# Hybrid decoder block on one core: gate and up as one level of Strassen's product, down as a stage of its own, full-height indexer matmuls

## The chip, the core and the metric

The kernel runs on one NeuronCore of one Trainium2 chip. A core has a matmul engine (TensorE, "PE" in the profile, with its weight loads listed as "PEld"), three elementwise engines (VectorE "DVE", ScalarE "ACT", GpSimd "POOL") and DMA queues, of which SyncE's ("SP") carries nearly all the transfers here. Every engine executes its own list of instructions in order; engines wait for each other through semaphores. The metric is the device time of one execution in microseconds (us). Lower is better.

## What is computed

The reference is one decoder block on 1024 tokens of width 1024, all in float32. What matters here is its last sub-layer and one piece of its first:

```
def _swiglu(h, w_gate_up, w_down):                 # D_FF = 2816
    g, u = jnp.split(h @ w_gate_up, 2, axis=-1)
    return (jax.nn.silu(g) * u) @ w_down
...
x = x + _rmsnorm(_swiglu(_rmsnorm(x, norm_ffn_pre), w_gate_up, w_down), norm_ffn_post)
...
dots = einsum('bthd,bsd->bths', q_idx, k_idx)      # indexer: 4 heads of 64 channels
score = einsum('bths,bth->bts', relu(dots), w_idx) # then top 256 keys per query
```

Ahead of the feed-forward layer stand the mixer sub-layer (one wide projection, causal pooling, the indexer with its top-256 selection, sparse attention, gating) and a cross-attention over 256 memory tokens.

## The kernel before

**Three matmuls for one product.** Every float32 operand is split into a high part of the reduced type `fp32r` and the rest, `lo = x - hi`. `split` (line 369) does it with one ACT copy and one DVE subtraction; `mm3` (line 425) then multiplies hi·hi, hi·lo and lo·hi, three matmuls of the fast type, into one PSUM bank. `wcols` and `wsplit` (lines 408 to 423) load and split a 128-column stripe of weights. So each product of a 128x128 weight block and 512 tokens is three 128x512 matmuls.

**The order is planned, not written.** `Recorder` (lines 54 to 329) collects every instruction with what it reads and writes, gives each a cost (`_cost`, line 185), and plays a list schedule: whichever engine is free takes the earliest recorded instruction that is ready by the model's clock and has room for its tiles. The result is one fixed order for each engine. Costs only decide this order. Big SBUF tiles (4 KB in each partition) come from one pool of `NSLOT` = 39 slots (tag "b", line 352); an instruction that opens such a tile may be taken at most `AHEAD` = 700 (or `SHORT` = 200) instructions ahead of the oldest one not yet planned. Four buffers of tag "ld" hold loads; PSUM is four single banks and two pairs of banks.

**The indexer** (lines 542 to 595). `kih` holds the high part of the keys in rows 0 to 63 and a copy in rows 64 to 127; `qi[h]` holds a head's high part in one half of the rows and its low part in the other; the copies between halves are DMAs issued from POOL (lines 552, 553, 564). `do_scores` then does one matmul over all 128 rows, which gives hi·hi + lo·hi, and one over 64 rows (`qi[h][pr]`, `kil[pr]`, line 587), which adds hi·lo, for each segment of keys. ACT applies the relu and DVE the weighted sum. The top-256 search that follows runs on DVE in the background of later projections.

**The end of the memory sub-layer.** `mem_out(b)` (line 1004) makes the 24 matmuls of token block b (tile `z`); `close` (line 930) is the chain that follows: ACT sums squares (`j_pb`), POOL makes the factor, DVE applies it (`zb`), POOL adds the residual (`zb` again), ACT sums squares (`j_nb`), POOL makes the factor, DVE applies it (`xn_nb`), and `norm_T` (line 444) makes eight PE transposes (`pt_nb`) whose result is split into `h3T`, the FFN's input: hidden channels by tokens, in two halves of 512 tokens (`HalfT`, line 455). Half 0 needs blocks 0 to 3 only.

**The feed-forward layer** (lines 1042 to 1105). For each stripe f of the 22 stripes of 128 hidden columns: gate (`o_g`), two token halves of 8 chunks by three matmuls, silu on ACT, the same for up (`o_up`), the product on DVE, a split into `aT`. After two stripes (four for the last piece) the `dn` matmuls multiply them with the rows of `w_down` and DVE adds the result to eight accumulators `acc`. The last piece also normalises, adds the residual and stores.

Of the kernel before, what the change touches and what calls it, by code (L numbers as in the profile page):

```python
# [10 lines left out]
F32 = mybir.dt.float32  # L11
F32R = mybir.dt.float32r
# [5 lines left out]
P = 128  # L18
# [35 lines left out]
class Recorder:  # L54
# [286 lines left out]
def hybrid_block_kernel(ctx: ExitStack, tc: tile.TileContext, x, mem, norm_mix_pre, norm_mix_post,  # L341
# [24 lines left out]
    def f32(t):  # L366
        return t.bitcast(F32)
# [76 lines left out]
    def norm_T(src, g, dst, name, eng=None):  # L444
        r = rstd_of(src, name)
        xn = slot([P, D], F32, f"xn_{name}")
        apply_norm(xn, src, r, g, eng)
        for q in range(2):
            pt = bank([P, 4, P], f"pt_{name}{q}")
            for c in range(4):  # L450
                nc.tensor.transpose(pt[:, c], xn[:, (4 * q + c) * P:(4 * q + c + 1) * P], ident)
            for (hi, lo, a, b) in dst(q):
                split(hi, lo, pt[:, a:b])

    class HalfT:
# [21 lines left out]
        def tok(self, b, c):  # L477
            h, t = divmod(b, 4)
            s = slice(t * P, (t + 1) * P)
            return self.hi[h][c // 2][:, c % 2, s], self.lo[h][c // 2][:, c % 2, s]  # L480

    class QuartT:
        def __init__(self, name):
            self.hi = [[None] * 2 for _ in range(4)]
# [59 lines left out]
    kih, kil = slot([P, S], F32R, "kih"), slot([P, S], F32R, "kil")  # L544
    qi = [slot([P, S], F32R, f"qi{m}") for m in range(IDXH)]
    for h in range(2):
        o = gemm_half(*wki[0], hT, h, "ki", (0, 512) if h else (0, 256, 512))
        s = slice(h * 512, (h + 1) * 512)
        nc.scalar.activation(kih[:64, s], o[:64], AF.Copy)
        nc.vector.tensor_tensor(kil[:64, s], o[:64], f32(kih[:64, s]), op=OP.subtract)  # L550
# [24 lines left out]
    def do_scores(i):  # L575
        n = (i + 1) * P
        off, segs = qk_cols(n)
        sc = slot([P, S], F32, f"score{i}")
        score[i] = sc
        qs = slice(i * P, (i + 1) * P)  # L580
        for h in range(IDXH):
            pr = slice((h % 2) * 64, (h % 2) * 64 + 64)
# [12 lines left out]
        nc.gpsimd.affine_select(sc[:, i * P:n], sc[:, i * P:n], pattern=[[-1, P]], compare_op=OP.is_ge,  # L595
                                fill=LOW, base=0, channel_multiplier=1)
# [331 lines left out]
                mm3(o[:, n], ah, al, w[c][0][:, ns], w[c][1][:, ns], c == 0, c == nk - 1)  # L928

    def close(o, res, dram, b, gpost, gpre, dst, name):  # L930
        of = o.rearrange("p n f -> p (n f)")
# [25 lines left out]
    h3T = HalfT("h3")  # L957
    oT = {}

    def mem_soft(u):  # L960
# [78 lines left out]
    pend()  # L1039


    g6 = gain(norm_ffn_post, "g6")
    acc = [None] * NB
    NF = DFF // P
    pieces = [range(f, f + 2) for f in range(0, NF - 4, 2)] + [range(NF - 4, NF)]
    for fs in pieces:
        f0 = fs[0]
        aT = {}
        for f in fs:
            gh, gl = wcols(w_gate_up, f * P, f"wg{f}")  # L1050
            sl = []
            for h in range(2):
                o = gemm_half(gh, gl, h3T, h, f"g{f}")
                t = slot([P, 512], F32, f"sl{f}{h}")
                nc.scalar.activation(t, o, AF.Silu)
                sl.append(t)
            uh, ul = wcols(w_gate_up, DFF + f * P, f"wu_{f}")
            for h in range(2):
                o = gemm_half(uh, ul, h3T, h, f"up{f}")
                nc.vector.tensor_tensor(sl[h], o, sl[h], op=OP.mult)  # L1060
                a = slot([P, 2, 512], F32R, f"aT{f}{h}")
                split(a[:, 0], a[:, 1], sl[h])
                aT[f, h] = a
        wd = {}
        for f in fs:
            wd[f] = wsplit(wload(w_down[f * P:(f + 1) * P, :], f"wd{f}"), f"wd{f}", keep=True)
        last = fs[-1] == NF - 1
        for b in range(NB):
            h, t = divmod(b, 4)
# [68 lines left out]
```

## Time and profile before

| what | value |
|---|---|
| median of the runs | 1693.86 us (1693.0 to 1694.52, 3 runs) |
| profiled execution | 1692.59 us |
| its span, first to last instruction | 1690.7 us |
| mean granted TensorE clock | 0.995 |
| busy: PE, DVE, ACT, POOL | 1647.9, 920.8, 511.7, 256.7 us |
| DMA moved | 148.10 MB, mean 88 GB/s |

How to read it: matmuls are pipelined, and the profile gives each a duration of about 389 ns although in a stream one starts every 227 ns; so the distance between starts, not the duration, is what a matmul costs. In the tables a group is named by its output and inputs, for example `o_g<-h3h,h_wg`. Nearly all instructions carry the recorder's line 139, so tiles, not lines, tell them apart.

### The profile page before, as it was taken

The page shows a single profiled execution, that of the slowest core. Times are in us where ns is not written, and L with a number is a line of the kernel's source. Part 1 is how long each engine was busy: PE and PEld are TensorE (multiplying, and loading weights), DVE is VectorE, ACT ScalarE, POOL GpSimd, SP SyncE. Part 2 cuts the span into 40 slices and gives each one's busy share as a digit, 9 for nine tenths or more (in the row PEclk, how much of TensorE's full clock was granted, in tenths as well). Part 3 has the DMA queues.
Part 4 walks back from the last instruction along what each step waited for, and adds up shares of the span by engine and source line. Part 5 has one row for each costly group of instructions (what it writes and reads, how often), then busy time and mean ns, then how long its engine had stood idle before and what let it go on. Part 6 is the DMA issues. An engine that isn't in the chain of part 4 may idle for free.

```text
span 1690.7 us, 20048 instructions
## 1 busy us (share of the span) xinstructions
PE 1647.9 (97%) x7854; PEld 1369.4 (81%) x7854; DVE 920.8 (54%) x1617; ACT 511.7 (30%) x914; POOL 256.7 (15%) x337
## 2 busy tenths in 40 slices
PE   6999999999999999999999999999999999999997
PEld 5667888887887888778898888888888888888886
DVE  6489999981178598464356533323324323323236
ACT  6442111223256267343346521121111111111222
POOL 5133000200044223013314600000000000000003
PEclk9999999999999999999999999999999999999999
DMA  7221222246341540385332421111121121110204
GB/s 215 60 63 37 68 83 63 87 101 192 100 163 51 162 131 1 112 282 167 112 96 80 162 75 50 28 60 50 38 63 50 38 63 49 39 50 26 61 27 149
DMA packets 155343, 148.10 MB, mean 88 GB/s; under 512 B 6129, under 2 KB 130801, under 8 KB 155249
## 3 DMA queue, kind: packets, MB, share of 16 engines
q1 hardware_dynamic: 154288, 145.51, 28.1%
q0 software_dynamic: 960, 1.31, 0.4%
q8 instruction: 62, 1.02, 0.3%
q14 instruction: 33, 0.26, 0.0%
HBM read 114.56 MB, written 30.93 MB: 86 GB/s over the span
## 4 chain that ended last, share of the span: by engine, by line
PE 85%; DVE 6%; DMA 4%; ACT 2%; issue 2%; POOL 1%; SPq 0%; DVEq 0%; POOLq 0%; ACTq 0%
PE o_up L139 14%; PE o_g L139 14%; PE dn L139 14%; PE o_gp L139 5%; PE o_ga L139 5%; PE o_pa L139 4%; PE y L139 4%; PE po L139 3%; PE z L139 3%; PE ap L139 3%; PE lg L139 2%; PE qm L139 2%; PE o_q L139 2%; DMA r_wga<-in_w_in_dram 2%; PE sc L139 2%
## 5 line engine op out<-in xcount | busy, mean ns | idle before, releaser
L139 PE MATMUL dn<-h_wd,aT 128*128 128x512 f32 x704 | 218.4, 389 | 0.0
L139 DVE TENSOR_SCALAR_CACHE_REDUCE tja<-score,canda 128x384 bf16<-128x384 f32 (+1 forms) x186 | 165.6, 942 | 0.9
L139 PEld LDWEIGHTS dn<-h_wd,aT 128*128 128x128 f32 x704 | 132.1, 188 | 27.4
L139 DVE TENSOR_TENSOR acc<-dn,acc 128x1024 f32<-128x1024 f32 (+1 forms) x80 | 89.4, 1118 | 89.1 <-PE dn L139 88.9
L139 PE MATMUL o_g<-h3h,h_wg 128*128 128x512 f32 x352 | 137.1, 389 | 0.0
L139 PE MATMUL o_g<-h3l,h_wg 128*128 128x512 f32 x352 | 137.1, 389 | 0.0
L139 PE MATMUL o_g<-h3h,l_wg 128*128 128x512 f32 x352 | 137.0, 389 | 0.0
L139 PE MATMUL o_up<-h3l,h_wu 128*128 128x512 f32 x352 | 137.0, 389 | 0.0
L139 PE MATMUL o_up<-h3h,l_wu 128*128 128x512 f32 x352 | 136.9, 389 | 0.0
L139 PE MATMUL o_up<-h3h,h_wu 128*128 128x512 f32 x352 | 136.9, 389 | 0.0
L139 PE MATMUL dn<-l_wd,aT 128*128 128x512 f32 x352 | 136.9, 389 | 0.0
L139 POOL TENSOR_SCALAR mef<-ms,ms 128x1 f32<-128x1 f32 x8 | 10.6, 1326 | 699.8 <-ACT jf L139 699.8
L139 DVE TENSOR_TENSOR sl<-o_up,sl 128x512 f32<-128x512 f32 x44 | 30.4, 692 | 139.4 <-PE o_up L139 139.4
L139 DVE TENSOR_TENSOR l_wg<-r_wg,h_wg 128x1024 fp32r<-128x1024 f32 x22 | 27.0, 1225 | 137.3 <-ACT h_wg L139 137.3
L139 ACT ACTIVATE sl<-o_g 128x512 f32<-128x512 f32 x44 | 26.0, 590 | 242.9 <-PE o_g L139 242.9
L139 PEld LDWEIGHTS o_g<-h3l,h_wg 128*128 128x128 f32 x352 | 66.1, 188 | 14.1 <-DVE h3l L139 0.4
L139 PEld LDWEIGHTS o_g<-h3h,h_wg 128*128 128x128 f32 x352 | 66.1, 188 | 13.8
L139 PEld LDWEIGHTS dn<-l_wd,aT 128*128 128x128 f32 x352 | 66.1, 188 | 13.7
L139 PEld LDWEIGHTS o_up<-h3l,h_wu 128*128 128x128 f32 x352 | 66.1, 188 | 13.7
L139 PEld LDWEIGHTS o_up<-h3h,l_wu 128*128 128x128 f32 x352 | 66.1, 188 | 13.7
L139 PEld LDWEIGHTS o_up<-h3h,h_wu 128*128 128x128 f32 x352 | 66.1, 188 | 13.7
L139 PEld LDWEIGHTS o_g<-h3h,l_wg 128*128 128x128 f32 x352 | 66.1, 188 | 13.7
(310 smaller groups left out, 3878.3 us busy)
## 6 DMA issues: line engine op xcount, KB each, us to landing
r_wg<-in_w_gate_up_dram SPq DMA_DIRECT2D x22, 512.0 KB, 3.8
r_wu<-in_w_gate_up_dram SPq DMA_DIRECT2D x22, 512.0 KB, 3.9
r_wd<-in_w_down_dram SPq DMA_DIRECT2D x22, 512.0 KB, 3.5
r_wpa<-in_w_proj_attn_dram SPq DMA_DIRECT2D x16, 512.0 KB, 3.7
x<-in_x_dram SPq DMA_DIRECT2D x8, 512.0 KB, 5.8
r_wgp<-in_w_in_dram SPq DMA_DIRECT2D x8, 512.0 KB, 4.4
mAd<-mA SPq DMA_DIRECT2D x8, 512.0 KB, 2.8
r_wq<-in_w_in_dram SPq DMA_DIRECT2D x8, 512.0 KB, 4.4
```

Of the source, the lines that this page charges most:

```text
L139: op.emit = lambda: fn(*args, **kw)
```

## The change

1. **Gate and up by seven products.** With A the weights (rows of A: gate stripe, up stripe; its columns: the first and second four chunks of hidden channels) and B the input (rows: the same two halves of the channels; columns: the even and the odd token blocks), the 2x2 product needs eight block products of 4 chunks by 512 tokens; Winograd's form of Strassen's method needs seven, and sums of blocks. `WinoT` replaces `HalfT` for `h3T`: it keeps each block's transposes in float32, forms T1 to T4 from each pair of blocks (on POOL, for the last pair on DVE), and `spread` splits the seven types into hi and lo. `units(f)` loads both stripes, forms S1 to S4 on POOL and splits seven weight blocks. `gate_up(f)` makes the seven products (`gab`, `gc`), adds them up in PSUM and on DVE, and writes silu(g)·u to DRAM (`aTd`).
2. **Down is a stage of its own** after all gate and up: pieces of 2, 4, 4, 4, 4, 4 stripes, with `aT` read back from DRAM and split there.
3. **Indexer.** `kil` becomes two tiles with zeros in the other 64 rows, so the second matmul runs over all 128 rows; the copies between halves are issued from SP.
4. **Planner and memory.** New costs for matmuls, ACT and DVE; `NSLOT` 42; a smaller scratch area for DMA descriptors.

```diff
-            return (n / 2.4 + 2.5) * (1 if n >= 256 else 4), 0.0
+            return n * 0.43 + 7.0, 0.0
-            return 60 + 0.85 * big + (110 if kw.get("accum_out") is not None else 0), 0.0
+            return 150 + 0.89 * big + (190 if kw.get("accum_out") is not None else 0), 0.0
-                return 130 + 1.04 * big, 0.0
-            return 70 + (0.56 if fast else 1.04) * big, 0.0
+                return 280 + 1.05 * big, 0.0
+            return 130 + (0.56 if fast else 1.06) * big, 0.0
-    NSLOT, LD = 39, 4
+    NSLOT, LD = 42, 4
+    class WinoT:
+        TYPES = ("B11", "T2", "T1", "T3", "B21", "T4", "B22")
...
+            xt = self.x[b] = slot([P, KC, P], F32, f"{self.name}x{b}")
...
+                nc.scalar.activation(xt[:, 4 * q:4 * q + 4], pt, AF.Copy)
+            if b % 2:
+                self.combine(b // 2)
+        def combine(self, u):
...
+            e = nc.vector if u == NB // 2 - 1 else nc.gpsimd
+            e.tensor_tensor(T1, B12, B11, op=OP.subtract)
+            e.tensor_tensor(T2, B22, T1, op=OP.subtract)
+            e.tensor_tensor(T3, B22, B12, op=OP.subtract)
+            e.tensor_tensor(T4, B21, T2, op=OP.subtract)
+        def spread(self):
+            for t in self.TYPES:
...
+                for u in range(NB // 2):
+                    s = slice(u * P, (u + 1) * P)
+                    for j in range(2):
+                        split(self.hl[t][0][j][:, :, s], self.hl[t][1][j][:, :, s], self.src[u][t][:, 2 * j:2 * j + 2])
-        nc.gpsimd.dma_start(kih[64:, s], kih[:64, s])
-        nc.gpsimd.dma_start(kil[64:, s], kil[:64, s])
+        nc.sync.dma_start(f32(kih)[64:, s], f32(kih)[:64, s])
+        nc.sync.dma_start(f32(kil[1])[64:, s], f32(kil[0])[:64, s])
-                nc.gpsimd.dma_start(q[other, s], lo[me, t0:])
+                nc.sync.dma_start(f32(q)[other, s], f32(lo)[me, t0:])
-                nc.tensor.matmul(oc, qi[h][pr, qs], kil[pr, c0:c1], start=False, stop=True)
+                nc.tensor.matmul(oc, qi[h][:, qs], kil[h % 2][:, c0:c1], start=False, stop=True)
+    def mmk(o, wh, wl, act, t, first):
+        for c in range(4):
+            ah, al = act.k(t, c)
+            nc.tensor.matmul(o, wh[:, c], ah, start=first and c == 0, stop=False, skip_group_check=True)
+            nc.tensor.matmul(o, wh[:, c], al, start=False, stop=False, skip_group_check=True)
+            nc.tensor.matmul(o, wl[:, c], ah, start=False, stop=c == 3, skip_group_check=True)
+    def units(f):
...
+        split(gh, gl, rg)
+        nc.gpsimd.tensor_tensor(S1, A21, A22, op=OP.add)
+        nc.gpsimd.tensor_tensor(S2, S1, A11, op=OP.subtract)
+        nc.gpsimd.tensor_tensor(S3, A11, A21, op=OP.subtract)
+        nc.gpsimd.tensor_tensor(S4, A12, S2, op=OP.subtract)
...
+        split(h12, l12, s12)
+        split(h34, l34, s34)
+        split(a22[:, 0], a22[:, 1], A22)
+    def gate_up(f, W):
...
+        prod(A, "A11", "B11", True)
+        nc.scalar.activation(m1, A, AF.Copy)
+        prod(B, "S2", "T2", True)
+        nc.vector.tensor_tensor(u2, B, m1, op=OP.add)
+        prod(C, "S1", "T1", True)
+        prod(B, "S3", "T3", False)
+        nc.vector.tensor_tensor(u3, B, m1, op=OP.add)
+        nc.vector.tensor_tensor(c22, C, u3, op=OP.add)
+        prod(A, "A12", "B21", False)
+        nc.scalar.activation(u3, A, AF.Silu)
+        prod(B, "A22", "T4", False)
+        nc.vector.tensor_tensor(c21, B, m1, op=OP.add)
+        nc.vector.tensor_tensor(c21, c21, u3, op=OP.mult)
+        nc.sync.dma_start(aTd[f, :, 0], c21)
+        prod(C, "S4", "B22", False)
+        nc.vector.tensor_tensor(c12, C, u2, op=OP.add)
+        nc.scalar.activation(c12, c12, AF.Silu)
+        nc.gpsimd.tensor_tensor(c12, c12, c22, op=OP.mult)
+        nc.sync.dma_start(aTd[f, :, 1], c12)
+    nxt = units(0)
+    for f in range(NF):
+        cur, nxt = nxt, units(f + 1) if f + 1 < NF else None
+        gate_up(f, cur)
-    pieces = [range(f, f + 2) for f in range(0, NF - 4, 2)] + [range(NF - 4, NF)]
+    pieces = [range(0, 2)] + [range(f, f + 4) for f in range(2, NF, 4)]
```

More of the change, by code (lines that the diff above doesn't have):

```diff
@@ L480, in tok, with __init__, k, close @@
             return self.hi[h][c // 2][:, c % 2, s], self.lo[h][c // 2][:, c % 2, s]
+    class WinoT:
+        TYPES = ("B11", "T2", "T1", "T3", "B21", "T4", "B22")
+        def __init__(self, name):
+            self.name, self.x, self.hl, self.src = name, {}, {}, {}
+        def k(self, t, c):
+            return self.hl[t][0][c // 2][:, c % 2], self.hl[t][1][c // 2][:, c % 2]
+        def close(self, src, g, b, name):
+            r = rstd_of(src, name)
+            xn = slot([P, D], F32, f"xn_{name}")
+            apply_norm(xn, src, r, g)
+            xt = self.x[b] = slot([P, KC, P], F32, f"{self.name}x{b}")
+            for q in range(2):
+                pt = bank([P, 4, P], f"pt_{name}{q}")
+                for c in range(4):
+                    nc.tensor.transpose(pt[:, c], xn[:, (4 * q + c) * P:(4 * q + c + 1) * P], ident)
+                nc.scalar.activation(xt[:, 4 * q:4 * q + 4], pt, AF.Copy)
+            if b % 2:
+                self.combine(b // 2)
+        def combine(self, u):
+            x0, x1 = self.x[2 * u], self.x[2 * u + 1]
+            B11, B21, B12, B22 = x0[:, :4], x0[:, 4:], x1[:, :4], x1[:, 4:]
+            t13, t24 = slot([P, 2, 4, P], F32, f"{self.name}s{u}"), slot([P, 2, 4, P], F32, f"{self.name}t{u}")
+            T1, T3, T2, T4 = t13[:, 0], t13[:, 1], t24[:, 0], t24[:, 1]
+            e = nc.vector if u == NB // 2 - 1 else nc.gpsimd
[3 more added lines that the diff above has]
+            e.tensor_tensor(T4, B21, T2, op=OP.subtract)
+            self.src[u] = dict(B11=B11, B21=B21, B22=B22, T1=T1, T2=T2, T3=T3, T4=T4)
+        def spread(self):
+            for t in self.TYPES:
+                self.hl[t] = [[slot([P, 2, 512], F32R, f"{self.name}{t}{v}{j}") for j in range(2)] for v in "hl"]
+                for u in range(NB // 2):
+                    s = slice(u * P, (u + 1) * P)
+                    for j in range(2):
+                        split(self.hl[t][0][j][:, :, s], self.hl[t][1][j][:, :, s], self.src[u][t][:, 2 * j:2 * j + 2])
     class QuartT:
@@ L543, in hybrid_block_kernel @@
     ki = slot([P, S], F32, "ki")
-    kih, kil = slot([P, S], F32R, "kih"), slot([P, S], F32R, "kil")
+    kih, kil = slot([P, S], F32R, "kih"), [slot([P, S], F32R, f"kil{r}") for r in range(2)]
+    nc.gpsimd.memset(f32(kil[0])[64:], 0.0)
+    nc.gpsimd.memset(f32(kil[1])[:64], 0.0)
     qi = [slot([P, S], F32R, f"qi{m}") for m in range(IDXH)]
@@ L549, in hybrid_block_kernel @@
         nc.scalar.activation(kih[:64, s], o[:64], AF.Copy)
-        nc.vector.tensor_tensor(kil[:64, s], o[:64], f32(kih[:64, s]), op=OP.subtract)
+        nc.vector.tensor_tensor(kil[0][:64, s], o[:64], f32(kih[:64, s]), op=OP.subtract)
         nc.scalar.activation(ki[:, s], o, AF.Copy)
-        nc.gpsimd.dma_start(kih[64:, s], kih[:64, s])
-        nc.gpsimd.dma_start(kil[64:, s], kil[:64, s])
+        nc.sync.dma_start(f32(kih)[64:, s], f32(kih)[:64, s])
+        nc.sync.dma_start(f32(kil[1])[64:, s], f32(kil[0])[:64, s])
         for m in range(2):
@@ L581, in do_scores @@
         for h in range(IDXH):
-            pr = slice((h % 2) * 64, (h % 2) * 64 + 64)
             o = bank2([P, S], f"sc{i}{h}")
@@ L930, in close @@
     def close(o, res, dram, b, gpost, gpre, dst, name):
+        wino = isinstance(dst, WinoT)
         of = o.rearrange("p n f -> p (n f)")
@@ L937, in close @@
         nc.sync.dma_start(dram[b * P:(b + 1) * P, :], z)
+        if wino:
+            return lambda: dst.close(z, gpre, b, f"n{name}{b}")
         return lambda: norm_T(z, gpre, dst.block(b), f"n{name}{b}")
@@ L956, in hybrid_block_kernel @@
     qml = [slot([P, MH, 256], F32R, f"qml{u}") for u in range(4)]
-    h3T = HalfT("h3")
+    h3T = WinoT("h3")
     oT = {}
@@ L1039, in hybrid_block_kernel @@
     pend()
+    h3T.spread()
+    NF = DFF // P
+    aTd = nc.tile(dr, [NF, P, 2, 512], F32, name="aTd", tag="aTd", dram=True)
+    def mmk(o, wh, wl, act, t, first):
+        for c in range(4):
+            ah, al = act.k(t, c)
+            nc.tensor.matmul(o, wh[:, c], ah, start=first and c == 0, stop=False, skip_group_check=True)
+            nc.tensor.matmul(o, wh[:, c], al, start=False, stop=False, skip_group_check=True)
+            nc.tensor.matmul(o, wl[:, c], ah, start=False, stop=c == 3, skip_group_check=True)
@@ new lines, in units @@
+    def units(f):
+        rg = wload(w_gate_up.rearrange("(k p) n -> p k n", p=P)[:, :, f * P:(f + 1) * P], f"wg{f}")
+        ru = wload(w_gate_up.rearrange("(k p) n -> p k n", p=P)[:, :, DFF + f * P:DFF + (f + 1) * P], f"wu_{f}")
+        A11, A12, A21, A22 = rg[:, :4], rg[:, 4:], ru[:, :4], ru[:, 4:]
+        nc.ahead = nc.SHORT
+        s12 = slot([P, 2, 4, P], F32, f"s12_{f}")
+        s34 = slot([P, 2, 4, P], F32, f"s34_{f}")
+        S1, S2, S3, S4 = s12[:, 0], s12[:, 1], s34[:, 0], s34[:, 1]
+        gh = nc.tile(sb, [P, KC, P], F32R, name=f"h_wg{f}", tag="whi", bufs=2)
+        gl = nc.tile(sb, [P, KC, P], F32R, name=f"l_wg{f}", tag="wlo", bufs=2)
+        split(gh, gl, rg)
[3 more added lines that the diff above has]
+        nc.gpsimd.tensor_tensor(S4, A12, S2, op=OP.subtract)
+        h12, l12 = slot([P, 2, 4, P], F32R, f"h12_{f}"), slot([P, 2, 4, P], F32R, f"l12_{f}")
+        split(h12, l12, s12)
+        h34, l34 = slot([P, 2, 4, P], F32R, f"h34_{f}"), slot([P, 2, 4, P], F32R, f"l34_{f}")
+        split(h34, l34, s34)
+        a22 = slot([P, 2, 4, P], F32R, f"a22_{f}")
+        split(a22[:, 0], a22[:, 1], A22)
+        nc.ahead = nc.AHEAD
+        return dict(A11=(gh[:, :4], gl[:, :4]), A12=(gh[:, 4:], gl[:, 4:]), A22=(a22[:, 0], a22[:, 1]),
+                    S1=(h12[:, 0], l12[:, 0]), S2=(h12[:, 1], l12[:, 1]),
+                    S3=(h34[:, 0], l34[:, 0]), S4=(h34[:, 1], l34[:, 1]))
@@ new lines, in gate_up, with prod @@
+    def gate_up(f, W):
+        ab = bank2([P, 2, 512], f"gab{f}")
+        A, B, C = ab[:, 0], ab[:, 1], bank([P, 512], f"gc{f}")
+        t0 = nc.tile(sb, [P, 2, 512], F32, name=f"gm{f}", tag="ld", bufs=LD)
+        t1 = nc.tile(sb, [P, 2, 512], F32, name=f"gu{f}", tag="ld", bufs=LD)
+        t2 = nc.tile(sb, [P, 2, 512], F32, name=f"gv{f}", tag="ld", bufs=LD)
+        m1, u2, u3, c22, c12, c21 = t0[:, 0], t0[:, 1], t1[:, 0], t1[:, 1], t2[:, 0], t2[:, 1]
+        def prod(o, a, t, first):
+            mmk(o, *W[a], h3T, t, first)
+        prod(A, "A11", "B11", True)
[17 more added lines that the diff above has]
+        nc.sync.dma_start(aTd[f, :, 1], c12)
@@ L1042, in hybrid_block_kernel @@
+    nxt = units(0)
+    for f in range(NF):
+        cur, nxt = nxt, units(f + 1) if f + 1 < NF else None
+        gate_up(f, cur)
     g6 = gain(norm_ffn_post, "g6")
     acc = [None] * NB
-    NF = DFF // P
-    pieces = [range(f, f + 2) for f in range(0, NF - 4, 2)] + [range(NF - 4, NF)]
+    pieces = [range(0, 2)] + [range(f, f + 4) for f in range(2, NF, 4)]
     for fs in pieces:
         f0 = fs[0]
[L1048 to L1064, printed above, removed]
+        aT, wd = {}, {}
@@ L1065, in hybrid_block_kernel @@
         for f in fs:
             wd[f] = wsplit(wload(w_down[f * P:(f + 1) * P, :], f"wd{f}"), f"wd{f}", keep=True)
+            at = nc.tile(sb, [P, 2, 512], F32, name=f"at{f}", tag="ld", bufs=LD)
+            nc.sync.dma_start(at, aTd[f])
+            nc.ahead = nc.SHORT
+            aT[f] = slot([P, 2, 512], F32R, f"aTh{f}"), slot([P, 2, 512], F32R, f"aTl{f}")
+            split(*aT[f], at)
+            nc.ahead = nc.AHEAD
         last = fs[-1] == NF - 1
         for b in range(NB):
-            h, t = divmod(b, 4)
+            t, h = divmod(b, 2)
@@ L1078, in hybrid_block_kernel @@
                 for f in fs:
-                    mm3(o[n], aT[f, h][:, 0, qs], aT[f, h][:, 1, qs], wd[f][0][:, ns], wd[f][1][:, ns],
+                    mm3(o[n], aT[f][0][:, h, qs], aT[f][1][:, h, qs], wd[f][0][:, ns], wd[f][1][:, ns],
                         f == fs[0], f == fs[-1])
@@ L1122 @@
     from concourse.bass_utils import run_bass_kernel_spmd as _run
-    nc = _bacc.Bacc("TRN2", target_bir_lowering=False, num_devices=1)
+    nc = _bacc.Bacc("TRN2", target_bir_lowering=False, num_devices=1, dynamic_dma_scratch_size=1024)
     arrays, args = {}, []
```

## The prediction

> **What bounds the kernel now.** I read the page's first part, then the chain that ended last, then the busy time by stretches.
>
> ```profile
> span 1690.7 us, 20048 instructions
> PE 1647.9 (97%) x7854; PEld 1369.4 (81%) x7854; DVE 920.8 (54%) x1617; ACT 511.7 (30%) x914; POOL 256.7 (15%) x337
> PE 85%; DVE 6%; DMA 4%; ACT 2%; issue 2%; POOL 1%; SPq 0%; DVEq 0%; POOLq 0%; ACTq 0%
> ```
>
> PE carries 85% of the chain. Within the feed-forward layer it carries all of it; in order of time the chain reads:
>
> ```profile
> 1029.33 10.88 PE o_g L139 x48
> 1040.21 10.88 PE o_up L139 x48
> ...
> 1072.85 21.76 PE dn L139 x96
> 1094.61 10.88 PE o_g L139 x48
> ```
>
> 48 matmuls of 128x512 take 10.88 us, 0.2267 us each, and one piece follows the other without a gap (1029.33 to 1094.61 is 65.28 us for 288 matmuls, again 0.2267). The busy time by stretches (columns: PE, PEld, DVE, ACT, POOL, granted clock, DMA share, GB/s) says the same of the whole layer, and how idle the others are:
>
> ```profile
> 1029.00:1638.00 609.00, 609.00 (x2689) 504.26 (x2687) 202.04 (x201) 103.96 (x136) 0.00 (x0) 1.00 0.16 48
> ```
>
> So in this layer the time is the number of matmuls, and the other engines have room: DVE is busy 33%, ACT 17%, POOL not at all.
>
> **The seven products.** Six gate and up groups of the page, of which these are the first and the last, hold 352 matmuls each:
>
> ```profile
> L139 PE MATMUL o_g<-h3h,h_wg 128*128 128x512 f32 x352 | 137.1, 389 | 0.0
> L139 PE MATMUL o_up<-h3h,h_wu 128*128 128x512 f32 x352 | 136.9, 389 | 0.0
> ```
>
> That is 2112. After the change, each of 22 stripes has 7 products of 4 chunks by 3 matmuls, all 128x512: 22 x 84 = 1848. The 264 that go are worth 264 x 0.2267 = 59.8 us. The down matmuls stay the same in number and shape.
>
> This holds only if PE does not wait for what was added. Per stripe PE has 84 x 0.2267 = 19.0 us. The prices:
>
> ```profile
> L139 DVE TENSOR_TENSOR l_wg<-r_wg,h_wg 128x1024 fp32r<-128x1024 f32 x21 | 25.7, 1225 | 136.8 <-ACT h_wg L139 136.8
> L139 DVE TENSOR_TENSOR sl<-o_up,sl 128x512 f32<-128x512 f32 x44 | 30.4, 692 | 139.4 <-PE o_up L139 139.4
> L139 ACT ACTIVATE h_wg<-r_wg 128x1024 fp32r<-128x1024 f32 x21 | 22.3, 1061 | 88.2 <-PE o_g L139 69.7 <-issue 18.6
> L139 ACT ACTIVATE sl<-o_g 128x512 f32<-128x512 f32 x44 | 26.0, 590 | 242.9 <-PE o_g L139 242.9
> DMA packets 155343, 148.10 MB, mean 88 GB/s; under 512 B 6129, under 2 KB 130801, under 8 KB 155249
> L139 POOL TENSOR_TENSOR mb<-Bn,mask 128x512 f32<-128x512 f32 x2 | 2.3, 1160 | 68.8 <-PE pt_nk L139 67.6 <-DMA Bn<-rowd 1.2
> ```
>
> DVE: three splits of 1.225, one of 0.69, six sums of 0.69: 8.5 us. ACT: three copies of 1.06 and four of 0.59: 5.5 us. POOL: five operations of 1.16: 5.8 us. DMA: two stripes and half a megabyte of results, 1.5 MB per 19 us or 80 GB/s, less than the mean over the whole span. All lie under the 19.0 us and are prepared one stripe ahead, so I cost them at nothing; if that cover went, POOL's S1, S2 and the split behind them (1.16 + 1.16 + 1.06 + 1.23 = 4.6 us, less the 2.7 us of a first product) would be late by 1.9 us a stripe, 42 us in all. Inside a stripe, bank B is read by DVE (0.69 us) and written again one product (2.7 us) later; one 1.2 us split queued ahead on DVE still fits. I take 0, with up to 0.3 us a stripe, 7 us, for the upper end.
>
> SP gains waits: a store of `aTd` waits for DVE or POOL, and behind it stand the stripe loads, which are a stripe ahead. Down reads stripes 0 and 1 back some 380 us after they were written. A piece of four needs 16 slots for weights and `aT`; with eight accumulators and the next piece that is 40 of 42, so pieces can be prepared one ahead: DVE 8 splits and 8 sums of 1.225, 19.6 us, under 192 x 0.2267 = 43.5 us of PE. At nothing; the tail (last piece of four stripes) is the same as before.
>
> **The indexer matmuls.** Starts on PE:
>
> ```profile
> 59.74 0.28 PE L139 MATMUL o_u<-hTh,h_wu 128*128 128x256 f32 x1
> 59.86 0.28 PE L139 MATMUL o_u<-hTl,h_wu 128*128 128x256 f32 x1
> ...
> 62.36 0.50 PE L139 MATMUL sc<-kil,qi 64*128 64x512 f32 x1
> 62.79 0.49 PE L139 MATMUL sc<-kih,qi 128*128 128x512 f32 x1
> 63.22 0.49 PE L139 MATMUL sc<-kil,qi 64*128 64x512 f32 x1
> ...
> 67.27 0.38 PE L139 MATMUL sc<-kih,qi 128*128 128x256 f32 x1
> 67.58 0.38 PE L139 MATMUL sc<-kil,qi 64*128 64x256 f32 x1
> L139 PE MATMUL sc<-kil,qi 64*128 64x512 f32 (+2 forms) x40 | 18.2, 455 | 0.0
> L139 PE MATMUL sc<-kih,qi 128*128 128x512 f32 (+2 forms) x40 | 17.1, 427 | 0.0
> ```
>
> In alternation with 64-row matmuls a 512-wide one starts every 0.43 us instead of 0.2267, a 256-wide one every 0.31 instead of 0.12: 0.2 us more, whichever of the two it is. I read this as a price of each change of height. Without changes of height 80 x 0.2 = 16 us of PE time go. The Trainium skill, "TensorE: Matmul & The Clock Gate", in its table under "Why this matters for your kernels", has a matmul of few rows take the same time as one of 128 rows; read alone, that makes this edit worth nothing, and the sum below would end 13 us higher. The trace speaks against it for this alternation.
>
> What is late next is DVE:
>
> ```profile
> 58.00:98.00 40.00, 40.00 (x144) 22.98 (x143) 26.41 (x38) 20.28 (x28) 4.55 (x8) 1.00 0.07 20
> 98.00:162.00 64.00, 60.69 (x261) 48.14 (x261) 61.40 (x109) 22.30 (x29) 28.51 (x28) 1.00 0.15 42
> ```
>
> The scores take 40 us in which DVE works 26.4; the stage cannot shrink below that, and in the stage behind it DVE works 61.4 of 64 us and cannot catch up. So 40 - 26.4 = 13.6 us at most by that path, 16 if PE finds projections to run ahead with, 8 if DVE's order fits badly. I take 13. The copies moved from POOL to SP and the zeros on POOL lie in the first 60 us beside other work: nothing.
>
> **Into the feed-forward layer.** Here the change costs time. Before, PE goes straight on:
>
> ```profile
> 959.78 0.39 PE L139 MATMUL z<-h_wom,oTl 128*128 128x512 f32 x1
> 960.01 1.04 PE L139 MATMUL pt_nb<-ident,xn_nb 128*128 128x128 f32 x8
> 960.80 0.48 PE L139 MATMUL o_g<-h3h,h_wg 128*128 128x512 f32 x1
> 966.12 1.04 PE L139 MATMUL pt_nb<-ident,xn_nb 128*128 128x128 f32 x8
> 971.67 1.06 PE L139 MATMUL pt_nb<-ident,xn_nb 128*128 128x128 f32 x8 [0.65 <-DVE xn_nb L139]
> L139 ACT ACTIVATE h3h<-pt_nb 128x256 fp32r<-128x256 f32 x20 | 6.0, 390 | 10.1 <-PE pt_nb L139 10.1
> L139 DVE TENSOR_TENSOR h3l<-pt_nb,h3h 128x256 fp32r<-128x256 f32 x4 | 1.4, 418 | 1.5 <-ACT h3h L139 1.5
> ```
>
> The last `z` matmul starts at 959.78, gate of half 0 at 960.80, and the transposes of blocks 6 and 7 come at 966.1 and 971.7, because the chain ACT, POOL, DVE, POOL, ACT, POOL, DVE takes some 11 us a block. Half 0 is the cover. After the change the even blocks form one column half: the first product needs block 6, two of the seven types (B11, B21) need block 6, the other five block 7. First product: 966.1, copy 0.59, high part 0.39, hops: about 968. Second product: 971.7, copy 0.6, T1 and T2 on DVE 1.4, split 0.8, hops 0.8: about 976. From 960.8 to 976 PE has two sets of transposes (1.6) and the first product of stripes 0 and 1 (5.4): 8.2 us idle, 6.4 if a product with B21 fits in too. Before it lost about 1.3. That is +5 to +7 with the chain undisturbed. It will be disturbed:
>
> ```profile
> 946.00:960.00 14.00, 14.00 (x67) 11.59 (x66) 8.11 (x13) 6.07 (x15) 10.31 (x11) 1.00 0.43 152
> 946.49 2.42 POOL L139 TENSOR_TENSOR zb<-zb,resb 128x1024 f32<-128x1024 f32 x1 [1.40 <-DVE zb L139]
> 958.65 3.37 POOL L139 TENSOR_TENSOR zb<-zb,resb 128x1024 f32<-128x1024 f32 x1 [0.36 <-DVE zb L139]
> ```
>
> POOL works 10.3 of 14 us here and gets the sums T1 to T4 of two pairs, 8 x 1.16 = 9.3 us, of which 3.7 fit; the residual adds, on the chain, come up to 5.6 us later, and they already stretch from 2.42 to 3.37 us beside DVE. DVE gets 56 halves of splits of 0.418, 23.4 us, part of them before 976, part just ahead of the products that need them. I take +12 for the passage; bounds +5 (only the longer wait for block 7) and +22 (all the 9.3 us late and half the rest of the splits uncovered).
>
> **The planner.** Old costs give a 128x1024 DVE operation 1135 ns, the new ones 1215, against 1225 in the row above; a 128x512 matmul 216, now 227, against 226.7. The order changes everywhere. The largest waits of PE behind the start are
>
> ```profile
> PE pt_nk L139 <- ACT q L139: 3.5, 1, 3.5
> PE lg L139 <- DVE mx L139: 3.2, 1, 3.2
> PE mx L139 <- ACT ph L139: 2.8, 2, 2.1
> ```
>
> and eleven smaller rows of that table bring them to 17.5 us. A truer plan may regain some or open others: bounds -10 and +8, I take -3, a sixth of them.
>
> **Sum.** The profiled execution took 1692.59 us, of which 1690.7 is the span; it lies 1.3 below the median of 1693.86. 1692.6 - 59.8 - 13 + 12 - 3 = 1628.8, so 1629, or 1630 beside the median.
>
> **The rivals.**
> - *The height costs nothing by itself* (the slow pace of `sc` has another cause, such as the alternating operands, which stays). For it: the row only shows alternation, and the page's sentence above. Against it: `o_u` alternates operands as well, at full pace. 1629 + 13 = 1642.
> - *The passage is worse.* DVE and POOL hold up each other over 23.4 + 9.3 us of sums and splits and the types come one by one: +25 instead of +12: 1642. For it: the stretched adds. Against it: DVE is idle 42% of 946 to 960 and may split early.
> - *PE stumbles inside the stripes*: the second use of banks A, B and C waits 0.5 us per stripe: 22 x 0.5 = 11: 1640. Against it: 2.7 us lie between.
> - *Slots run out, and it is slower.* The seven types hold 28 of 42 slots for the whole stage, a stripe in use 5, the next 7 while it is made: 40. If the planner cannot open the next stripe's tiles before the present one ends, each stripe begins with load, S1, S2, split, S4, split in a row: 4 x 1.16 + two splits of 2.3 = 9.2 us, less 2.7 of the first product, 6.5 x 22 = 143 us: 1772. It decides from 64 / 22 = 2.9 us a stripe. Against it: two slots are left over, and the sums of a stripe give theirs back.
>
> **Chances.** The forecast 0.62, no gain in the indexer 0.08, a worse passage 0.15, stumbling 0.11, no slots 0.04. All but the last are far below the time before: faster by over 0.2% 0.95, within 0.2% (3.4 us, about what a measurement of this kernel can tell from no change) 0.01, slower 0.04. Range: down to 1612 (indexer -16, passage +5, planner -10 would give 1609; I leave out 3, since not all come together), up to 1653 (the passage at +25 and a stumble of 11 on top).
>
> **What would show it.** Right: 1848 matmuls in `gab` and `gc`, a stripe every 19.0 us without PE waits; `sc` 512 wide at 0.23 us; between the last `z` and the second product some 8 to 15 us of PE idle, ended by POOL or DVE; `dn` gapless. Wrong: `sc` still at 0.43; PE idle before each stripe, ended by an `s12`, `h12` or `l12` tile; a `dn` piece waiting for `aT`.

## The result: slower, not faster

The kernel after took 1714.99 us (median of 4 runs, 1714.11 to 1715.95), the kernel before 1694.19 us beside it (4 runs, 1693.0 to 1696.05): ratio 1.0122, 95% interval 1.0104 to 1.0139. The forecast was 1629 us, with a range of 1612 to 1653.

The head of the page of the kernel after:

```profile
span 1714.2 us, 20275 instructions
PE 1602.8 (94%) x7590; PEld 1317.5 (77%) x7590; DVE 1032.3 (60%) x1723; ACT 578.7 (34%) x1000; POOL 436.7 (25%) x449
```

PE has 264 matmuls fewer (7854 before) and is busy 45 us less, as was intended; yet the span is 23.5 us longer. PE must be waiting. The chain that ended last shows where (start, length, engine, tile, instructions). The first part is one stripe in the middle of the layer, the last line the down stage:

```profile
1097.01 2.72 PE gc L139 x12
1099.73 2.96 PE gab L139 x13
...
1102.71 0.70 DVE gu L139
...
1103.46 3.98 PE gab L139 x16
...
1107.46 0.61 ACT gu L139
...
1108.11 1.88 PE gab L139 x7
1109.99 2.72 PE gc L139 x12
1112.71 3.87 PE gab L139 x17
...
1116.60 0.61 ACT gm L139
...
1117.25 1.88 PE gab L139 x7
1119.13 2.72 PE gc L139 x12
...
1466.61 239.37 PE dn L139 x1056
```

Read the counts. Down is gapless: 239.37 / 1056 = 0.2267 us. But in the stripe the chain leaves PE three times, once for DVE and twice for ACT, for 0.6 or 0.7 us each. Product 5 (`A12` by `B21`, into bank A) is cut after its first matmul: 13 is the twelve of product 4 and one more. Products 6 and 2, into bank B, are cut after five of twelve. From `gc` to `gc` a stripe takes 1119.13 - 1097.01 = 22.12 us, where 84 x 0.2267 = 19.04 was reckoned: 3.08 us are lost, in 22 stripes 68 us. (The first two stripes lose more, because the passage into the layer reaches into them.)

The waits of PE (waiting tile, releaser: us in total, times, longest):

```profile
PE gab L139 <- DVE gu L139: 18.9, 21, 3.2
PE gab L139 <- ACT gu L139: 16.5, 22, 1.9
PE gab L139 <- ACT gm L139: 14.9, 21, 1.2
PE pt_nb L139 <- DVE xn_nb L139: 13.1, 3, 6.5
```

The first three rows make 50.3 us, each row about once a stripe. The rest of the 68 lies around each stop, which costs more than its recorded wait. PE's own order around two of them:

```profile
1124.41 0.39 PE L139 MATMUL gab<-h3B21h,h_wg 128*128 128x512 f32 x1
1125.58 0.50 PE L139 MATMUL gab<-h3B21l,h_wg 128*128 128x512 f32 x1 [0.78 <-DVE gu L139]
...
1137.14 0.39 PE L139 MATMUL gab<-h3B11h,l_wg 128*128 128x512 f32 x1
1137.36 0.39 PE L139 MATMUL gab<-h3T2h,h 128*128 128x512 f32 x1
```

and ACT's copy `m1` of bank A in the second place:

```profile
1138.69 0.60 ACT L139 ACTIVATE gm<-gab 128x512 f32<-128x512 f32 x1 [0.54 <-PE gab L139]
```

The matmul at 1125.58 writes bank A, and waits for a DVE instruction that reads bank **B**; it starts 1.17 us after the one before, 0.94 over the pace, where the row says 0.78. The copy of bank A needs only the matmul of 1137.14, which is through some 0.4 us later, and ACT itself is free at 1138.15 (1138.69 less the 0.54 us of idle time). It starts at 1138.69, when five matmuls into bank **B**, from 1137.36 on, are through as well (1137.36 + 4 x 0.2267 + 0.39 = 1138.66). A and B are not two tiles: the code has `ab = bank2(...)`, `A, B = ab[:, 0], ab[:, 1]`. The reader of one half waits for the matmuls into the other half that stand ahead of it in the program, and the next matmul into the other half waits for that reader. The recorder does not know of this: it compares regions of a tile (`_hit`), so by its plan A and B are independent, and it puts matmuls into one half ahead of a reader of the other.

With the last `y` matmul as a mark, the difference of the two spans splits like this. The last `y` and the last `dn` before:

```profile
833.02 0.40 PE L139 MATMUL y<-h_wo,mgl 128*128 128x512 f32 x1
1681.74 0.39 PE L139 MATMUL dn<-h_wd,aT 128*128 128x512 f32 x1
```

and after:

```profile
818.63 0.39 PE L139 MATMUL y<-h_wo,mgl 128*128 128x512 f32 x1
1705.58 0.39 PE L139 MATMUL dn<-h_wd,aTl 128*128 128x512 f32 x1
```

Ahead of the mark 14.4 us are gained. Behind it stand 848.72 us before, less 59.85 for the matmuls 788.87; after has 886.95, or 98.1 too much: 68 in the stripes, and 30 in the passage into the layer and just ahead of it. -14.4 - 59.85 + 98.1 = +23.9, against 23.5 of the spans. Below, "excess" is always this: last `y` to last `dn` in the profiled execution, less 788.87 (848.72 in a kernel without the seven products).

### The profile page after: what moved, and what is told of

Its sections match the earlier page's. It is cut to its first block, busy times and chain, and to the rows that moved or that the text cites. A ratio compares the mean times of both kernels' runs of the same rounds, so it can differ in the third digit from the quotient of the medians.

```text
span 1714.2 us, 20275 instructions
## 1 busy us (share of the span) xinstructions
PE 1602.8 (94%) x7590; PEld 1317.5 (77%) x7590; DVE 1032.3 (60%) x1723; ACT 578.7 (34%) x1000; POOL 436.7 (25%) x449
## 5 line engine op out<-in xcount | busy, mean ns | idle before, releaser
L139 PE MATMUL dn<-h_wd,aTh 128*128 128x512 f32 x352 | 136.8, 389 | 0.0
L139 PE MATMUL dn<-l_wd,aTh 128*128 128x512 f32 x352 | 136.8, 389 | 0.0
L139 PE MATMUL dn<-h_wd,aTl 128*128 128x512 f32 x352 | 136.6, 389 | 0.0
L139 DVE TENSOR_TENSOR l<-s,h 128x1024 fp32r<-128x1024 f32 x44 | 54.1, 1232 | 43.4 <-PE gc L139 32.7
L139 PEld LDWEIGHTS dn<-h_wd,aTh 128*128 128x128 f32 x352 | 66.1, 188 | 13.8
L139 PEld LDWEIGHTS dn<-l_wd,aTh 128*128 128x128 f32 x352 | 66.1, 188 | 13.7
L139 PEld LDWEIGHTS dn<-h_wd,aTl 128*128 128x128 f32 x352 | 66.1, 188 | 13.7
L139 PE MATMUL gab<-h3T4h,a 128*128 128x512 f32 x176 | 61.2, 408 | 15.0 <-ACT gu L139 15.0
L139 POOL TENSOR_SCALAR mef<-ms,ms 128x1 f32<-128x1 f32 x8 | 10.6, 1328 | 224.2 <-ACT jf L139 224.2
L139 PE MATMUL lg<-kTh,qq 128*128 128x512 f32 (+2 forms) x192 | 61.4, 363 | 3.3 <-DVE my L139 1.6
L139 PE MATMUL po<-T,Vh 128*128 128x512 f32 x144 | 55.4, 419 | 3.8 <-DVE nm L139 1.6
```

The lines of the kernel that those rows point to most:

```text
L139: op.emit = lambda: fn(*args, **kw)
```

## The experiments

The theory to be tested: waits are kept per tile, and the pair tile costs 68 us; the passage into the layer costs some 30. The rival for the first: the second use of each bank comes too early for its reader, whatever the tile.

**A and B in tiles of their own** (the kernel after, one line):

```diff
-        ab = bank2([P, 2, 512], f"gab{f}")
-        A, B, C = ab[:, 0], ab[:, 1], bank([P, 512], f"gc{f}")
+        A, B, C = bank([P, 512], f"ga{f}"), bank2([P, 2, 512], f"gb{f}")[:, 0], bank([P, 512], f"gc{f}")
```

> The changed kernel with one edit: the sums A and B of a stripe lie in two PSUM tiles instead of the two halves of one. Theory (waits are kept per tile, so a reader of A waits for matmuls into B and the next matmul into B waits for that reader): the three waits per stripe go, a stripe falls from 22.1 to 19.0 us, 22 x 3.1 = 68 us less, 1715 - 68 = 1647 us. Rival 1 (the waits are true ones: each bank is written again before it is read): nothing changes, 1715. Rival 2 (DVE and POOL are too slow for the stripe, as the bound): the waits move to other tiles and less than 20 us go, above 1695.

1652.11 us, ratio to before 0.9749 (0.9733 to 0.9766): 63 us less than after. The same products in the same order, and the chain of this kernel is PE alone:

```profile
1031.11 2.72 PE gb L139 x12
1033.83 2.72 PE ga L139 x12
...
1050.15 2.72 PE gb L139 x12
1052.87 2.72 PE ga L139 x12
```

1050.15 - 1031.11 = 19.04 us a stripe. Bank B is written again after one product, as before, A and C after three; the same instructions read them, and PE does not wait: the rival falls. The excess drops from 98.1 to 31.8.

**The same fault put into the kernel before**: gate's two column halves get the two halves of one pair tile.

```diff
-    def gemm_half(wh, wl, act, h, name, cuts=(0, 512)):
-        o = bank([P, 512], f"o_{name}{h}")
+    def gemm_half(wh, wl, act, h, name, cuts=(0, 512), o=None):
+        o = bank([P, 512], f"o_{name}{h}") if o is None else o
...
+            pair = bank2([P, 2, 512], f"o_gp2{f}")
...
-                o = gemm_half(gh, gl, h3T, h, f"g{f}")
+                o = gemm_half(gh, gl, h3T, h, f"g{f}", o=pair[:, h])
```

> The kernel before with one edit: the two token halves of gate go to the two halves of one PSUM pair instead of two single banks. The same matmuls, readers and data. Theory (waits kept per tile): silu of half 0 waits for the matmul into half 1 that stands ahead of it, and the matmul after that waits for silu: one stop of about 0.9 us a stripe, 22 x 0.9 = 20 us more, 1714. Rival (a reader of one bank and a writer of the other do not disturb each other): 1694.

1713.62 us, 1.0113 (1.0096 to 1.013). The chain of this kernel:

```profile
1031.75 5.68 PE o_gp L139 x25
...
1037.45 0.60 ACT sl L139
...
1038.10 5.51 PE o_gp L139 x23
1043.61 10.88 PE o_up L139 x48
```

24 matmuls of half 0 and one of half 1, then PE waits for silu of half 0: 11.86 us (1031.75 to 1043.61) for what took 10.88, so 0.98 a stripe, 21.6 in 22; the excess is 20.3. Without any of the new method, the wait comes with the tile.

**The indexer alone** (the kernel before with point 3 of the change), and **all but the seven products** (the kernel before with points 3 and 4). One line of each part:

```diff
...
-                nc.tensor.matmul(oc, qi[h][pr, qs], kil[pr, c0:c1], start=False, stop=True)
+                nc.tensor.matmul(oc, qi[h][:, qs], kil[h % 2][:, c0:c1], start=False, stop=True)
...
```

```diff
...
-            return 70 + (0.56 if fast else 1.04) * big, 0.0
+            return 130 + (0.56 if fast else 1.06) * big, 0.0
...
-    NSLOT, LD = 39, 4
+    NSLOT, LD = 42, 4
...
```

> The kernel before with the indexer part alone (two zero-padded kil tiles, 128-row second matmul, copies from SP); old costs, 39 slots, no Strassen. Theory (each change between 64 and 128 rows costs PE 0.2 us): sc starts every 0.23 us at 512 wide, the scores end 13 to 17 us earlier and 12 to 16 us of it last to the end: 1694 - 14 = 1680. Rival (the height costs nothing by itself): sc stays at 0.43 us and the time at 1694.

> The kernel before with everything of the change but the seven products and the split of the layer: indexer part, new costs, 42 slots, small scratch. Theory: the planner is worth 3 us or less, so within 4 us of the indexer part alone, about 1677. Rival (the new plan itself costs time ahead of the feed-forward layer, which would be part of the loss): above 1685.

1678.47 us (0.991, 0.9895 to 0.9925) and 1679.0 us (0.9909, 0.9893 to 0.9924). The indexer is worth 16 us, the new costs and slots nothing that can be told from noise. The excess is 0.3 in both: neither touches what lies behind the last `y`.

The remaining 32 us of excess are the passage from the memory sub-layer to the first full stripe. With separate tiles, 6.6 of them lie ahead of the last `z` matmul (133.4 us from the last `y` to it, 126.8 before), 9.6 between it and the first gate product (10.6 us, 1.0 before), and the rest in the first two stripes, which take 33.2 and 23.6 us. Eight more kernels take apart what stands there.

A caution for all of them: this kernel, these eight and the kernel after have the same order of instructions on PE, DVE, ACT and POOL up to the last `y`, and yet it starts anywhere from 814.63 to 822.05 us. So totals that differ by a few us do not tell two of these kernels apart, and the excess, which leaves that stretch out, is one execution of each.

**Column halves of blocks 0 to 3 and 4 to 7**, so that the first half is complete before block 6 (on the kernel with separate tiles):

```diff
-            if b % 2:
-                self.combine(b // 2)
+            if b >= NB // 2:
+                self.combine(b - NB // 2)
...
-            x0, x1 = self.x[2 * u], self.x[2 * u + 1]
+            x0, x1 = self.x[u], self.x[u + NB // 2]
```

> The kernel with split banks, and the column halves made of blocks 0 to 3 and 4 to 7 instead of even and odd blocks (T1 to T4 from block u and block u + 4). It tests the lost cover: now B11 and B21 need blocks 0 to 3 only, so two of seven products of the first stripes (10.9 us for two stripes) can run while the last blocks are closed. If the passage is lost for want of cover: 1652 - 10 = 1642. If it is lost because DVE and POOL hold each other up (a 128x256 low part of 0.42 us takes 1.4 us beside POOL): no gain or a loss, 1650 to 1660, since all sums of T now fall into the last four blocks.

1652.87 us (0.9755, 0.9732 to 0.9777), excess 34.5: no gain. The cover did come back: the first gate product starts 0.23 us after the last `z` matmul. But the last block's transposes (`pt_nb`) come 34.2 us after that `z`, against 23.7 with even and odd blocks, since all T sums now fall into the last four blocks. What the cover alone is worth is not shown.

**All T sums on DVE** (on the kernel with separate tiles):

```diff
-            e = nc.vector if u == NB // 2 - 1 else nc.gpsimd
+            e = nc.vector
```

> The kernel with split banks, and T1 to T4 of all four block pairs on DVE instead of three pairs on POOL. If DVE and POOL hold each other up: DVE gets 12 x 0.69 = 8.3 us more but loses most of 17 us of stretched operations, POOL is free for the residual adds, 1652 - 9 = 1643. If the want of cover is what costs: DVE only gets more work, 1652 to 1660.

1643.76 us (0.9703, 0.968 to 0.9726), 8 us less, as expected. But look where. The profiled execution is the slowest of the four, 1647.57 us. DVE's low parts in the passage (936 to 994 us; busy, mean ns), with separate tiles and POOL making the sums:

```profile
L139 DVE TENSOR_TENSOR h3T1l<-h3s,h3T1h 128x256 fp32r<-128x256 f32 x6 | 8.3, 1411 | 1.8 <-ACT h3T1h L139 1.8
L139 DVE TENSOR_TENSOR h3T4l<-h3t,h3T4h 128x256 fp32r<-128x256 f32 x8 | 4.1, 545 | 0.0
```

and without POOL's sums:

```profile
L139 DVE TENSOR_TENSOR h3T4l<-h3t,h3T4h 128x256 fp32r<-128x256 f32 x8 | 6.1, 807 | 3.8 <-ACT h3T4h L139 3.8
L139 DVE TENSOR_TENSOR h3T1l<-h3s,h3T1h 128x256 fp32r<-128x256 f32 x6 | 2.4, 414 | 0.3 <-ACT h3T1h L139 0.3
```

The T1 splits fall from 1.41 to 0.41 us each, so POOL had held them up; but others now pay, and the excess only goes from 31.8 to 30.6. In the two profiled executions, 4.3 of the 5.5 us between the spans lie ahead of the last `y` (822.05 against 817.77), where the orders are the same and only the run differs. The total came out as expected; that the passage gave it is not shown.

**Both together** (the halves by blocks 0 to 3 and 4 to 7, and all T sums on DVE), and **S1 to S4 of stripes 0 and 1 on DVE too** (on the kernel with all T sums on DVE):

```diff
+        e = nc.vector if f < 2 else nc.gpsimd
-        nc.gpsimd.tensor_tensor(S1, A21, A22, op=OP.add)
+        e.tensor_tensor(S1, A21, A22, op=OP.add)
...
```

> Both edits: halves by blocks 0 to 3 and 4 to 7, and all T sums on DVE. If both causes hold and add up: 1652 - 19 = 1633. If the sixteen sums of the last four blocks now make DVE the bound: 1645 to 1660.

> The kernel with split banks, all T sums on DVE, and S1 to S4 of the first two stripes on DVE as well, so that POOL has only the residual adds in the passage. If the two engines holding each other up is what costs: some 3 to 5 us below the kernel with the T sums alone on DVE, 1639. If the amount of DVE work is what costs: 3 to 6 us above it.

1646.94 us (0.9715, 0.9695 to 0.9735), excess 30.4, and 1644.66 us (0.9703, 0.968 to 0.9726), excess 28.1. The first lies in the range of its second branch, the second in neither. The two edits do not add up. Beside the other halves, the T sums on DVE gave 5.9 us by the medians and 4.1 by the excess (34.5 to 30.4), so the gain of taking them from POOL came twice, but its size within the passage stays open. Moving POOL's first weight sums to DVE gives nothing in the total.

**The residual adds of blocks 4 to 7 on DVE**, and **the low parts left out** (matmuls that took a low part take the high part again). Both start from the kernel with all T sums on DVE:

```diff
-        nc.gpsimd.tensor_tensor(z, z, xb, op=OP.add)
+        (nc.vector if wino and b >= 4 else nc.gpsimd).tensor_tensor(z, z, xb, op=OP.add)
```

```diff
-                        split(self.hl[t][0][j][:, :, s], self.hl[t][1][j][:, :, s], self.src[u][t][:, 2 * j:2 * j + 2])
+                        nc.scalar.activation(self.hl[t][0][j][:, :, s], self.src[u][t][:, 2 * j:2 * j + 2], AF.Copy)
```

> The kernel with split banks and all T sums on DVE; in addition the residual add of blocks 4 to 7 ahead of the feed-forward layer goes from POOL (2.4 us and more) to DVE (about 1.25 us). If what is left of the passage is the two engines holding each other up: the chain of each block shortens by about 1.5 us and DVE's own stretched operations shrink, 1644 - 5 = 1639. If the amount of DVE work is what is left: 1644 to 1648.

> The kernel with split banks and all T sums on DVE, without the low parts of the feed-forward layer's input: the 56 subtractions of spread on DVE are left out and the matmuls that took a low part take the high part again, so that their number stays. If DVE's share of spread (56 x 0.42 = 23 us) is what PE waits for in the passage: most of the 25 us that PE loses there go, 1644 - 15 = 1629 or less. If the chain of the last blocks or the clock is what is left: 1640 to 1644.

1641.94 us (0.9694, 0.9674 to 0.9714) with an excess of 24.3; this is the lowest time of a complete kernel, though not apart from the one with all T sums on DVE. And 1646.78 us (0.9714, 0.9699 to 0.9728), excess 29.3, for the other: with 56 subtractions gone from DVE, nothing is gained, so DVE's splits were not the limit by themselves. (The edit also frees 14 slots, and the plan behind the last `y` changes with it.) What POOL does in that kernel:

```profile
958.87 1.74 POOL L139 TENSOR_TENSOR s<-r_wg,r_wu 128x512 f32<-128x512 f32 x1
960.70 0.54 POOL L139 TENSOR_SCALAR me_nb<-ms_nb 128x1 f32<-128x1 f32 x1
961.33 1.29 POOL L139 TENSOR_TENSOR s<-r_wg,s 128x512 f32<-128x512 f32 x1
962.57 1.02 POOL L139 TENSOR_TENSOR rs_nb<-me_nb,mhalf 128x1 f32<-128x1 f32 x1
```

`me_nb` and `rs_nb` are steps of the normalization of one of the last blocks, which PE waits for; the weight sums `s` of the first stripes stand before and between them in the same queue. ACT's sum of squares (`j_nb`), which this `me_nb` needs, is through at 957.4; it starts 3.3 us later.

**Without the early weight sums** (on the kernel with the residual adds on DVE; stripes 0 and 1 read the up stripe in their place), and **without the T sums too**:

```diff
-        nc.gpsimd.tensor_tensor(S1, A21, A22, op=OP.add)
-        nc.gpsimd.tensor_tensor(S2, S1, A11, op=OP.subtract)
...
+        if f < 2:
+            s12 = s34 = ru.rearrange("p (a b) n -> p a b n", a=2)
...
```

```diff
-            e.tensor_tensor(T1, B12, B11, op=OP.subtract)
-            e.tensor_tensor(T2, B22, T1, op=OP.subtract)
...
+            T1, T2, T3, T4 = B12, B22, B12, B22
```

> The kernel with split banks, T sums and late residual adds on DVE; the sums S1 to S4 of stripes 0 and 1 are left out (their splits read the up stripe itself), so that POOL has only the small factor steps and early residual adds in the passage. If POOL's S sums, standing between the chain's own POOL steps, are what delays blocks 6 and 7: 1642 - 7 = 1635. If not: 1640 to 1643.

> The same, and the sums T1 to T4 are left out too (the types take blocks of the input itself), so that no sum of Strassen's method is left in the passage, only the splits and the even and odd halves. If the sums on DVE are what is left: the passage falls to the undisturbed 7 us, 1642 - 16 = 1626. If the even and odd halves themselves (the wait for blocks 6 and 7) or the order of the plan cost more: 1632 to 1640.

1635.24 us (0.9652, 0.9637 to 0.9667), excess 16.7; and 1635.04 us (0.9654, 0.9638 to 0.967), excess 14.2. So the early S sums on POOL cost 7 us; the T sums, once on DVE, 2.5 us of excess and nothing in the median. What is left with all sums gone, on PE:

```profile
949.11 0.40 PE L139 MATMUL z<-h_wom,oTl 128*128 128x512 f32 x1
955.04 1.94 PE L139 MATMUL pt_nb<-ident,xn_nb 128*128 128x128 f32 x8 [5.54 <-DVE xn_nb L139]
959.01 1.22 PE L139 MATMUL ga<-h3B11h,h_wg 128*128 128x512 f32 x2 [2.03 <-ACT h3B11h L139]
960.03 0.63 PE L139 MATMUL ga<-h3B11l,h_wg 128*128 128x512 f32 x1
960.45 0.63 PE L139 MATMUL ga<-h3B11h,l_wg 128*128 128x512 f32 x1
```

PE waits 5.54 us for block 6, 2.03 for the high part of its B11, and then runs at 0.43 us a matmul for a while. By place, 2.6 of the 14.2 us lie ahead of the last `z` matmul, 8.9 between it and the first gate product, and 2.7 behind.

The traces also show where each edit acted. From the last `z` matmul to the last transposes is the chain of the last block; behind it PE can wait once more, in the first four stripes (all in us, one execution each; waits over 0.15 us):

| kernel | last `z` to last transposes | PE's waits in it | PE's waits behind it | excess |
|---|---|---|---|---|
| before | 11.9 | 0.6 | 0.0 | 0.0 |
| separate tiles | 23.7 | 12.2 | 3.8 | 31.8 |
| T sums on DVE | 26.5 | 12.4 | 3.9 | 30.6 |
| and S sums of stripes 0, 1 on DVE | 15.4 | 4.7 | 9.6 | 28.1 |
| T sums and residual adds on DVE | 20.0 | 14.5 | 2.6 | 24.3 |
| and without the early S sums | 12.9 | 9.5 | 2.1 | 16.7 |
| and without the T sums | 13.8 | 7.6 | 2.7 | 14.2 |

Without the early S sums the chain is 7.1 us shorter and the median 6.7 us lower: on POOL they delay the chain. Moved to DVE they no longer do (26.5 to 15.4), but PE waits 5.7 us more behind the chain, for splits and sums of the first stripes. That is where the gain of that edit went.

## Why the prediction was wrong, point by point

**The step that failed** is the one on the inside of a stripe. The prediction said: "Inside a stripe, bank B is read by DVE (0.69 us) and written again one product (2.7 us) later ... I take 0, with up to 0.3 us a stripe, 7 us, for the upper end." It reckoned with three banks that are waited for one by one. They are two tiles, and every reader of one half stands in the way of the matmuls into the other: three stops a stripe, 3.08 us, 68 us in all, shown from both sides by the separate tiles (-63 us, and 66 less excess) and by the pair put into the kernel before (one stop a stripe, +19 us). Of the 86 us between 1629 and 1715, 68 are this and 18 the passage. The rival "PE stumbles inside the stripes" named the place, but with its price of 0.5 us a stripe and the same false reason against it ("2.7 us lie between"). The point from which the change must lose, 2.9 us a stripe, stood in the text beside another mechanism; the pair passed it. In the kernel before every pair tile (`dn`, `y`, `z`, `lg`, `ml`, `sc`) is written to the end before it is read, so no row there had the price; but the code had the hint: where down's last piece reads the halves one by one, it takes two tiles of one bank each.

**The seven products**, -59.8: right. PE has 264 matmuls fewer, and with separate tiles a stripe takes the 19.04 us that was reckoned. The sums on DVE, ACT and POOL were hidden within the stripes, as said, though POOL's became dearer: `s<-r_wu` 1.515 us in the mean, not 1.16.

**The indexer**, -13: right, -16 by the medians and -13.6 at the last `y` (833.02 before, 819.38 with the indexer alone). In the kernel after:

```profile
60.65 0.40 PE L139 MATMUL sc<-kih,qi 128*128 128x512 f32 x1
60.88 0.39 PE L139 MATMUL sc<-kil,qi 128*128 128x512 f32 x1
61.11 0.40 PE L139 MATMUL sc<-kih,qi 128*128 128x512 f32 x1
```

0.23 us from start to start, 0.43 before, and the operands alternate as they did: the alternation of heights was the price. The rival that the height costs nothing falls. The Trainium skill, "TensorE: Matmul & The Clock Gate", "Why this matters for your kernels", which the prediction set beside it, speaks of a single matmul of few rows; it says nothing there of alternating heights, and could not price this edit.

**The planner**, -3: it was 0 within noise (1678.47 and 1679.0 us).

**The passage**, +12, at most +22: too low, 30 in the kernel after. The waits that the prediction named did come: 14.6 us between the last `z` and the second product, where it gave 8 to 15. What it left out lies around them. The S sums of the first stripes were reckoned as hidden; on POOL, among the steps of the normalization, they cost 7 us. The T sums on POOL cost 8.4 by the medians but 1.2 by the excess, the residual adds on POOL 6 by the excess (30.6 to 24.3) but 1.8 by the medians, which do not tell the two kernels apart; both sizes stay open. And no term was set down for the clock: from 940 to 1029 us, 21 of the 128x512 matmuls start 0.43 us after the one before without a wait of their own, 21 x 0.2 = 4.2 us. These costs overlap and do not add up to the 30. In the kernel after (columns as in the prediction's table by stretches):

```profile
946.00:960.00 14.00, 8.37 (x37) 6.75 (x35) 10.83 (x13) 7.63 (x18) 11.71 (x11) 0.74 0.19 77
960.00:976.00 16.00, 8.20 (x34) 6.09 (x34) 15.59 (x20) 10.18 (x23) 12.70 (x10) 0.82 0.19 66
976.00:1029.00 53.00, 44.16 (x170) 33.98 (x170) 35.21 (x41) 20.55 (x32) 31.30 (x18) 0.88 0.30 90
1029.00:1640.00 611.00, 568.35 (x2430) 451.22 (x2429) 271.63 (x270) 145.54 (x174) 130.86 (x89) 1.00 0.27 88
```

The granted clock is 0.74, 0.82 and 0.88 in the passage, where it was 1.00 before, and DVE works 15.59 of 16 us from 960 to 976. The rival of a worse passage (+25, from DVE and POOL holding up each other) had the size nearly right. Its mechanism is shown on single rows, 1.41 against 0.41 us; how much of the 30 it made is not shown, as said of the T sums.

With separate tiles the prediction's own sum, at the measured passage and planner, is 1692.6 - 59.8 - 16 + 32 = 1649, against 1652.11: apart from the pair and the passage nothing of size is missing. Without the pair the time lies in the forecast range by 1 us, but that is no credit to the sum, whose passage was 18 us too small: the range reached that far for a stumble of 11 us that is not there once the tiles are separate.

**Signs and sums.** Of the signs set down for being wrong, none showed: `sc` runs at 0.23 us, no stripe starts with a wait for its weight sums, `dn` is gapless. The fault lay where no sign had been set. And one sum is off: the lower end, 1692.6 - 59.8 - 16 + 5 - 10, is 1612, not 1609, so nothing was left out there.

## What to carry to other kernels

Where two accumulators share one tile, reckon each as if the other's readers were its own: write down for every tile, not for every bank, who reads it between which matmuls. A change that gives PE less work behind a chain of small steps takes away the cover of that chain; look at each queue that the chain passes through and at what the change puts ahead of its steps. And when an experiment's total comes out as expected, see in the profile whether it came from the place that the theory names.

## What the runs showed of the hardware

**The clock after a stop.** In the kernel after, the last matmuls of `z` around a stop:

```profile
940.94 0.39 PE L139 MATMUL z<-h_wom,oTl 128*128 128x512 f32 x1
944.31 0.61 PE L139 MATMUL z<-h_wom,oTh 128*128 128x512 f32 x1 [2.98 <-DVE zb L139]
944.71 0.63 PE L139 MATMUL z<-l_wom,oTh 128*128 128x512 f32 x1
945.14 0.63 PE L139 MATMUL z<-h_wom,oTl 128*128 128x512 f32 x1
```

After 3 us of waiting a matmul starts every 0.43 us, nearly twice the 0.2267, until 946.85; the granted clock is 0.59 in the mean from 944 to 947 and 1.00 from 938 to 944. The waits of 0.7 to 0.8 us in the stripes, three in each 22 us, leave the clock at 1.00 (the stretch from 1029 above). The Trainium skill, "TensorE: Matmul & The Clock Gate", "Why this matters for your kernels", warns of gaps of more than about 3 us, after which the clock is halved; the trace agrees, with 2.98 us.

**DVE beside POOL.** A DVE subtraction of 128x256 with both inputs in SBUF took 0.41 us where POOL ran nothing (17 of the 56 in the kernel with separate tiles, none over 0.42) and 0.97 in the mean, 2.6 at most, where POOL ran as well (the other 39). The Trainium skill, "SBUF — State Buffer", "Who interferes with whom", says that a DVE instruction with two SBUF inputs contends with a GpSimd instruction that reads SBUF; the trace agrees.
